# A layer's list scheduler gets longer step durations, and a stretch for VectorE beside GpSimd

## The chip, the core and the metric

The kernel runs on one core of a Trainium2 chip. The metric is the device time of one execution in microseconds (us). In the profile the engines are called PE (TensorE matmul), PEld (its weight loads), DVE (VectorE), ACT (ScalarE), POOL (GpSimd) and SP (SyncE, which issues most DMAs).

## What is computed

One decoder layer over 1024 tokens of width 1024, batch 1, float32:

```python
mod = silu(c) @ w_ada + b_ada            # -> sh1, sc1, gt1, sh2, sc2, gt2
h = rms_norm(x, g_pre_mix) * (1 + sc1) + sh1
proj = h @ w_in                          # -> u | bg | cg | v, 512 columns each
y_a = s5_mixer(u, ...)                   # 32 complex state spaces, GELU, sigmoid GLU
y_b = bg * causal_dwconv(cg * v, conv_w) # width 3
y = concat(head_rms_norm(y_a), head_rms_norm(y_b))
x = x + gt1 * rms_norm(y @ w_out, g_post_mix)
h = rms_norm(x, g_pre_ffn) * (1 + sc2) + sh2
a, v = split(causal_dwconv(h @ w_up, ffn_conv_w))
x = x + gt2 * rms_norm((silu(a) * v) @ w_down, g_post_ffn)
```

## The kernel before, in words

Everything lies with channels on the 128 partitions and tokens along the free axis, so x is 8 tiles (`x`, k = 0 to 7) of 128 x 1024. Every large product is made in three passes (`mm3`, the matmuls of L475, L477 and L479): both factors are split into a high and a low part, and high x high, high x low and low x high are added up in PSUM. PSUM has three buffers of 128 x 1024 (`big`) and two of 128 x 512 (`sm`). A weight tile is loaded by SP (`w`), cast to its high part by ACT (L461) and its low part taken by DVE or POOL (L381); it lies in one of three buffers `hl`.

The work up to about 560 us of the span runs in these stages, which overlap:

- **u product** (`t_u`): u = x @ w_in's first 512 columns, made from x scaled by its columns alone (`X`), with the token's norm applied afterwards (`t_u_out`). What the shift sh1 adds to it, the bias, is made per pair of tiles from the shift's high and low parts `shl` (L692 to L695, one column each) in `t_bias` (L801, L802): bias 0 to 3, each adding to `bs`, and at the end `bu` (L816, L818). A bias group frees the weight buffer that it shared with the u product. The last 512 tokens of the last 128 columns come behind, as `uh2`.
- **h** (`t_h`, L714 to L725): the normalised x with scale and shift, split in two parts.
- **projection** (`t_proj`): twelve products of h, the matmuls `big<-h,hl`, 48 each. The first two run in turns on two PSUM buffers. `t_conv` makes of each three of them a tile of group b: `p`, the taps on DVE, and at its end `yb` (L867), which frees the PSUM buffer.
- **tables of the state space**, made by POOL for four sets of eight groups: rotations `Pt`, `CL`, `WB`, and for the tap kernels `Bd` (L1072 to L1077), which PE multiplies (L1084, L1086, called taps here).
- **per set** (`t_set`): `V` (L1201, from u and the turned `WB`, L1126), four products on DVE that free its PSUM buffer (L867 `sv<-big,Pt`), a scan, `Y` (L1253, L1258), and GELU in two DVE steps (`z<-z,big`) and two of ACT.
- **GLU and norms**: `t_glu`, `t_gate`, the heads' statistics (L1378), and their expansion (L1421).
- **ada dots** (L631 on DVE, L633 on POOL): the columns of mod, one per 128 x 1024 tile of weights.
- **output product** (`big<-yh,hl`), then the channel sub-layer, whose products fill PE from about 560 us to the end.

The order is not written out by hand. Each piece of work above is a thread, a Python generator that yields a step (engine, planned duration) before it emits the step's instructions. `Flow` is a list scheduler: it keeps a planned time at which each engine is free, takes the engine and time at which the next step could start, and among the threads that could start within 0.02 us the one with the best number in `PRIO`. Waits for other threads, for buffers and for landed loads are planned too. Some steps may go to DVE or POOL (`SITES`), and go where they are planned to end first. The order in which `Flow` comes to the steps is the order of the instructions on each engine, and a step planned too late or too early stays there: each engine executes its queue in order. The durations come from `D_`, `A_` and `G_` (DVE, ACT and POOL, by the elements n per partition) and `M_` (PE).

Of the kernel before, what the change touches and what calls it, by code (L numbers as in the profile page):

```python
# [24 lines left out]
H = 512  # L25
# [176 lines left out]
class Flow:  # L202
# [85 lines left out]
    def run(self, until=None):  # L288

        while True:  # L290
            self._settle()
            if until is not None and until.t is not None:
                return
            ready = [th for th in self.threads if th[4][0] in ("run", "load", "pick")]
            if not ready:
                break
            plan = [(self._choice(th), th) for th in ready]
            t0, e = min((c[0], c[1]) for c, _ in plan)
            (start, e, cost), th = min(
                ((c, th) for c, th in plan if c[1] == e and c[0] <= t0 + 0.02), key=lambda p: p[1][:2]  # L300
            )
            end = self._pe_end(start, cost) if e == "pe" else start + cost
            self.free[e] = end
            if th[4][0] == "load":
                th[3] = start
                th[5] = end + LAND
            else:
                th[3] = end
            th[6] = e
            self._step(th, e if th[4][0] == "pick" else None)  # L310
        assert not self.threads, [(t[0], t[1], t[4], t[2].__name__, t[3]) for t in self.threads]
# [3 lines left out]
def hybrid_layer(ctx, tc, xT, w_adaT, w_ada0, w_u, w_bcv, w_out, w_up, w_down, glu_w, vec, ssm, con, out):  # L315
    nc = tc.nc
    outB = out.rearrange("(b p d) -> b p d", p=P, d=D)
    pe, dve, act, pool = nc.tensor, nc.vector, nc.scalar, nc.gpsimd
# [22 lines left out]
    def big(shape=(P, 1024)):  # L341
        return pbig.tile(list(shape), F32, tag="big", name=nm("big"))

    def small():
        return psm.tile([P, H], F32, tag="sm", name=nm("sm"))
# [7 lines left out]
    def k2(s="t"):  # L353
        return kp2.tile([P, H], F32, tag="k2", name=nm(s))
# [6 lines left out]


    def D_(n):
        return ("run", "dve", 0.07 + 1.04e-3 * n)

    def A_(n):
        return ("run", "act", 0.094 + 0.833e-3 * n)

    def G_(n):
        return ("run", "pool", 0.15 + 2.1e-3 * n)  # L370

    def M_(n):
        return ("run", "pe", n)
# [97 lines left out]
    def mm3(outs, wh, wl, xh, xl, start, stop):  # L471

        n = len(outs)
        for i in range(n):
            pe.matmul(outs[i], wh, xh[i], start=start, stop=False)  # L475
        for i in range(n):
            pe.matmul(outs[i], wh, xl[i], start=False, stop=False)  # L477
        for i in range(n):
            pe.matmul(outs[i], wl, xh[i], start=False, stop=stop)  # L479
# [257 lines left out]
    def t_u():  # L737
        yield ("wait", ev_X[0])
        yield ("get", "big", 3)
        yield ("get", "sm")  # L740
        up = [big() for _ in range(3)]
        uh = small()
        uo = [[t[:, :H], t[:, H:]] for t in up] + [[uh]]
        yield ("get", "k2")
        bs = k2("bs")[:2]
        for k in range(KD):
            yield ("wait", ev_X[k])
            w = wev["u", k // 2]
            yield ("wait", w[0])
            hl = w[1]  # L750
            for c4 in range(NT):
                n = len(uo[c4])
                o = (k % 2) * H + c4 * P
                if c4 == 0:
                    yield M_(0.215 * n)
                    for i in range(n):
                        pe.matmul(uo[0][i], hl[:, 0, o : o + P], X[k][0][i], start=k == 0, stop=False)
                    yield ("wait", ev_Xl[k])
                    yield M_(0.43 * n)
                    for i in range(n):  # L760
                        pe.matmul(uo[0][i], hl[:, 0, o : o + P], X[k][1][i], start=False, stop=False)
                    for i in range(n):
                        pe.matmul(uo[0][i], hl[:, 1, o : o + P], X[k][0][i], start=False, stop=k == KD - 1)
                else:
                    yield M_(0.6465 * n)
                    mm3(uo[c4], hl[:, 0, o : o + P], hl[:, 1, o : o + P], X[k][0][:n], X[k][1][:n], k == 0, k == KD - 1)
            fl.put("k2", 2)
            if k % 2:
                fl.spawn(t_bias(k // 2, hl, bs), PRIO["t_bias"])
        fl.fire(ev_u2)  # L770
        for c4 in (3, 0, 1, 2):
            fl.spawn(t_u_out(c4, uo[c4] + [None]), PRIO["t_u_out"])
        w = wev["u3",]
        yield ("wait", w[0])
        hl = w[1]
        yield ("get", "sm")
        uh2 = small()
        for k in range(KD):
            ks = slice(k * P, (k + 1) * P)
            yield M_(0.6465)  # L780
            mm3([uh2], hl[:, 0, ks], hl[:, 1, ks], X[k][0][1:], X[k][1][1:], k == 0, k == KD - 1)
            fl.put("k2", 2)
        fl.put("hl")
        fl.fire(ev_ups)
        ev_ups.tile = uh2
# [527 lines left out]
    def t_proj():  # L1313
        yield ("wait", ev_ups)

        for group in [bc_order[:PROJ_GROUP]] + [[t] for t in bc_order[PROJ_GROUP:]]:
            tiles_ = []
            for k in range(KD):
                ks = slice(k * P, (k + 1) * P)
                yield ("wait", ev_h[k])  # L1320
                for i, (n, c4) in enumerate(group):
                    if k == 0:
                        w = wev["p", n + c4]
                        yield ("wait", w[0])
                        yield ("get", "big")
                        tiles_.append((big(), w[1]))
                    o, hl = tiles_[i]
                    yield M_(1.293)
                    mm3([o[:, :H], o[:, H:]], hl[:, 0, ks], hl[:, 1, ks], hT[k][0], hT[k][1], k == 0, k == KD - 1)
            for (n, c4), (o, _) in zip(group, tiles_):  # L1330
                fl.put("hl")
                proj_ev[n + c4].tile = o
                fl.fire(proj_ev[n + c4])
        fl.put("k2", 4 * KD)
# [107 lines left out]
    def t_glu():  # L1442
        for s in range(NT):
            yield ("wait", sets[s]["z"])
        yield ("get", "sm")
        ev_stat["a"].tile = small()
        for c4 in range(NT):
            w = wev["g", c4 // 2]
            yield ("wait", w[0])
            gl = w[1]  # L1450
            yield ("get", "big")
            o = big()
            oo = [o[:, :H], o[:, H:]]
            for k in range(NT):
                ks = slice((c4 % 2) * H + k * P, (c4 % 2) * H + (k + 1) * P)
                yield M_(1.293)
                mm3(oo, gl[:, 0, ks], gl[:, 1, ks], zs[k][0], zs[k][1], k == 0, k == NT - 1)
            if c4 % 2:
                fl.put("hl")
            fl.spawn(t_gate(c4, o), PRIO["t_gate"])  # L1460
# [77 lines left out]
    def t_out():  # L1538
        for bi, (hf, lo, hi) in enumerate(blocks):
            n = hi - lo  # L1540
            outs, og4 = {}, {}
            so = [[], [Event() for _ in range(NT)]]
            for part, dp in w_seq[bi]:
                w = wev["o", bi - ((part, dp) in (kept(bi - 1) if bi else [])), part, dp]
                yield ("wait", w[0])
                hl = w[1]
                if part == first:
                    yield ("get", "big")
                    outs[dp] = big((P, 2, H))
                for k4_ in range(NT):  # L1550
                    k = k4_ + (0 if part == "A" else NT)
                    yield ("wait", ev_y[k][hf])
                    yield M_(1.293 * n / H)
                    for d2 in range(2):
                        ks = slice(k4_ * 256 + d2 * P, k4_ * 256 + (d2 + 1) * P)
                        mm3(
                            [outs[dp][:, d2, :n]], hl[:, 0, ks], hl[:, 1, ks], [yT[k][0][hf][:, lo:hi]], [yT[k][1][hf][:, lo:hi]],
                            part == first and k4_ == 0, part == last and k4_ == NT - 1,
                        )
                if (part, dp) not in kept(bi):  # L1560
                    fl.put("hl")
                if part == last:
                    og4[dp] = Event()
                    fl.spawn(t_out_evac(bi, n, dp, outs[dp], og4, so, len(og4) - 1), PRIO["t_out_evac"])
            if hi == H:
                fl.put("k2", 4 * KD // 2)
            fl.spawn(t_resid(bi, og4, so), PRIO["t_resid"])
        fl.fire(ev_out)
# [929 lines left out]
```

## Time and profile before

| | us |
|---|---|
| median of 3 runs | 1140.34 |
| lowest and highest | 1136.54, 1142.83 |
| the profiled execution | 1135.78 |
| its span | 1134.0 |
| PE busy | 1049.4 |
| DVE busy | 889.3 |
| ACT busy | 482.9 |
| POOL busy | 473.9 |

The clock granted to TensorE is 0.969 of full speed in the mean. Line 2 of the page cuts the span in 40 slices of 28.35 us; each digit is the busy share of a slice in tenths:

```profile
PE   2988889999897998898999999999999999999996
...
DVE  6769779777998288989888799788888887554763
ACT  4435412322344456565433333333334455454552
POOL 4799445671486134212343444343443220342002
PEclk9979889999898998999999999999999999999999
```

PE is nearly full from the twentieth slice on; ahead of it lie slices at 7 and 8 tenths, with a lower clock in some of them. DVE is at 9 tenths in the fourth slice and in the eleventh and twelfth, POOL in the third and fourth. The chain of waits on the page goes back to 934 us only and tells of the last product alone.

### The profile page before, as it was taken

What the parts mean: (1) busy time and instruction counts of PE and PEld (TensorE: products, weight loads), DVE (VectorE), ACT (ScalarE), POOL (GpSimd) and SP (SyncE); (2) the same over time, 40 slices, a digit from 0 to 9 for tenths busy, and PEclk for the clock granted to TensorE, in tenths of its full rate; (3) what the DMA queues carried; (4) which work ended last, traced back from release to release, by engine and by line L of the source; (5) the groups of instructions that cost most, each with busy time, mean ns of one, the idle gap of its engine ahead of it and who ended that gap; (6) DMA issues with size and microseconds to landing.
All of it is one profiled execution on the core that took longest, in us unless ns stands there. A gap on an engine that the chain in (4) does not pass through costs nothing. (4 is left out here: it accounts for less than half of the span.)

```text
span 1134.0 us, 13972 instructions
## 1 busy us (share of the span) xinstructions
PE 1049.4 (93%) x5012; PEld 848.6 (75%) x5012; DVE 889.3 (78%) x1218; ACT 482.9 (43%) x672; POOL 473.9 (42%) x469
## 2 busy tenths in 40 slices
PE   2988889999897998898999999999999999999996
PEld 2756677778554898687778888888888887888885
DVE  6769779777998288989888799788888887554763
ACT  4435412322344456565433333333334455454552
POOL 4799445671486134212343444343443220342002
PEclk9979889999898998999999999999999999999999
DMA  7633313236754356423552233223323597999337
GB/s 276 233 132 131 113 38 98 79 121 213 254 197 133 126 176 196 158 75 121 186 167 96 72 123 128 79 90 112 112 91 104 207 262 245 261 220 293 117 93 139
DMA packets 88821, 172.07 MB, mean 152 GB/s; under 512 B 8752, under 2 KB 34096, under 8 KB 88752
## 3 DMA queue, kind: packets, MB, share of 16 engines
q1 hardware_dynamic: 80688, 156.50, 41.0%
q0 software_dynamic: 8064, 14.68, 7.8%
q8 instruction: 39, 0.64, 0.2%
q14 instruction: 30, 0.25, 0.1%
HBM read 133.69 MB, written 37.46 MB: 151 GB/s over the span
## 5 line engine op out<-in xcount | busy, mean ns | idle before, releaser
L381 POOL TENSOR_TENSOR hl<-w,hl 128x1024 fp32r<-128x1024 f32 x40 | 102.9, 2575 | 284.7 <-ACT hl L1882 149.0
L381 POOL TENSOR_TENSOR w<-w,w 128x512 f32<-128x512 f32 x57 | 84.2, 1477 | 81.9 <-DVE hl L867 78.9
L1882 ACT CAST hl<-w 128x1024 fp32r<-128x1024 f32 (+1 forms) x65 | 66.5, 1023 | 47.7 <-issue 22.9
L2210 POOL DMA_DIRECT2D wd<-in_w_down_dram x44 | 38.5, 884 | 113.0 <-DMA wd<-in_w_down_dram 45.4
L867 DVE TENSOR_TENSOR wl<-wd,wh 128x512 fp32r<-128x512 f32 x77 | 50.9, 686 | 38.5 <-ACT wh L2214 38.2
L477 PE MATMUL big<-yl,hl 128*128 128x256 f32 (+1 forms) x192 | 63.4, 330 | 7.5 <-POOL yl L381 7.5
L2214 ACT CAST wh<-wd 128x512 fp32r<-128x512 f32 x77 | 46.1, 619 | 53.2 <-DMA wd<-in_w_down_dram 51.3
L870 DVE SCALAR_TENSOR_TENSOR ca<-big,vec,ca 128x896 f32<-128x896 f32 (+1 forms) x92 | 65.2, 740 | 3.2 <-ACT ca L2048 3.1
L475 PE MATMUL big<-h,hl 128*128 128x512 f32 x192 | 63.4, 412 | 3.3 <-ACT h L723 1.5
L867 DVE TENSOR_TENSOR hl<-w,hl 128x1024 fp32r<-128x1024 f32 (+1 forms) x45 | 52.9, 1174 | 16.4 <-ACT hl L1882 16.3
L461 ACT CAST hl<-w 128x1024 fp32r<-128x1024 f32 x43 | 44.9, 1044 | 48.0 <-PE big L479 31.2
L475 PE MATMUL big<-yh,hl 128*128 128x256 f32 (+1 forms) x192 | 64.9, 338 | 0.1
L477 PE MATMUL big<-h,hl 128*128 128x512 f32 x192 | 61.4, 401 | 3.0 <-DVE h L725 3.0
L479 PE MATMUL big<-h,hl 128*128 128x512 f32 x192 | 61.1, 400 | 2.8 <-POOL hl L381 2.8
L479 PE MATMUL big<-yh,hl 128*128 128x256 f32 (+1 forms) x192 | 63.3, 330 | 0.1
L475 PE MATMUL big<-s,hl 128*128 128x512 f32 x160 | 63.2, 395 | 0.0
L477 PE MATMUL big<-s,hl 128*128 128x512 f32 x160 | 63.0, 394 | 0.0
L479 PE MATMUL big<-s,hl 128*128 128x512 f32 x160 | 62.8, 393 | 0.0
L475 PE MATMUL big<-h2h,hl 128*128 128x512 f32 (+1 forms) x160 | 60.2, 376 | 0.0
L870 DVE SCALAR_TENSOR_TENSOR cv<-big,vec,cv 128x896 f32<-128x896 f32 (+1 forms) x84 | 58.5, 740 | 1.3 <-ACT cv L2048 1.3
L477 PE MATMUL big<-h2l,hl 128*128 128x512 f32 (+1 forms) x160 | 59.4, 372 | 0.0
L479 PE MATMUL big<-h2h,hl 128*128 128x512 f32 (+1 forms) x160 | 59.4, 372 | 0.0
(361 smaller groups left out, 3162.2 us busy)
## 6 DMA issues: line engine op xcount, KB each, us to landing
w<-in_w_up_dram SPq DMA_DIRECT2D x44, 512.0 KB, 4.0
w<-g_dr SPq DMA_DIRECT2D x35, 512.0 KB, 6.1
g_dr<-cv SPq DMA_DIRECT2D x53, 256.0 KB, 2.2
wd<-in_w_down_dram SPq DMA_DIRECT2D x44, 256.0 KB, 7.7
wd<-in_w_down_dram POOLq DMA_DIRECT2D x44, 256.0 KB, 6.5
w<-in_w_out_dram SPq DMA_DIRECT2D x20, 512.0 KB, 3.6
WBT<-in_w_adaT_dram SPq DMA_DIRECT2D x16, 512.0 KB, 4.6
w<-in_w_bcv_dram SPq DMA_DIRECT2D x13, 512.0 KB, 3.8
```

Of the source, the lines that this page charges most:

```text
L381: {"dve": dve, "pool": pool}[e].tensor_tensor(o, a, b, op)
L461: act.copy(t[:, 0, :], w)
L475: pe.matmul(outs[i], wh, xh[i], start=start, stop=False)
L477: pe.matmul(outs[i], wh, xl[i], start=False, stop=False)
L479: pe.matmul(outs[i], wl, xh[i], start=False, stop=stop)
L867: (eng or dve).tensor_tensor(o, a, b, op)
L870: dve.scalar_tensor_tensor(o, a, s, b, op0, op1)
L1882: act.copy(t[:, 0, :n], w)
L2210: pool.dma_start(w, block_of(made[1], kk), accum_op=ADD)
L2214: act.copy(hi, w)
```

## The change

The durations that the planner reckons with become longer, and a DVE step that is planned while POOL is planned to be busy counts 1.25 times. The constants of the channel sub-layer's steps stay as they were.

```diff
@@ Flow.run
+            if e == "dve" and self.free.get("pool", 0.0) > start:
+                cost *= 1.25
             end = self._pe_end(start, cost) if e == "pe" else start + cost
@@ D_, A_, G_
-        return ("run", "dve", 0.07 + 1.04e-3 * n)
+        return ("run", "dve", 0.155 + 1.045e-3 * n)
-        return ("run", "act", 0.094 + 0.833e-3 * n)
+        return ("run", "act", 0.19 + 0.84e-3 * n)
-        return ("run", "pool", 0.15 + 2.1e-3 * n)
+        return ("run", "pool", 0.18 + 2.2e-3 * n)
@@ t_u
-                    yield M_(0.6465 * n)
+                    yield M_(0.681 * n)
-            yield M_(0.6465)
+            yield M_(0.681)
@@ t_proj, t_glu
-                    yield M_(1.293)
+                    yield M_(1.362)
@@ the output product
-                    yield M_(1.293 * n / H)
+                    yield M_(1.362 * n / H)
```

PE has 4433 rows in both programs, DVE 1129 before and 1136 now, ACT 637 and 631, POOL 455 and 454. The new program's line numbers are 3 higher behind `Flow.run` (L1084 is L1087, L801 is L804). Its order differs from the old one in many places up to the channel sub-layer; three follow. Names end in the number of their buffer.

PE at the end of the u product, in before (from row 186): the last u matmul, bias 3, uh2, the column sums of the bias, the first h matmul, and 72 h matmuls later the taps.

```order
L479 MATMUL sm_243<-X_381,hl_431 128x512
L801 MATMUL sm_790<-hl_431,shl 2x512
...
L475 MATMUL sm_803<-X_225,hl_683 128x512
...
L816 MATMUL sm_816<-con,bs_244 128x1 x4
...
L475 MATMUL big_879<-h_749,hl_709 128x512
...
L1084 MATMUL sm_1037<-ssm,Bd_1017 32x16 x2
L1086 MATMUL sm_1037<-CL_848,Bd_1017 32x112 x2
```

The same place of PE now (from row 178): the last u matmul, the taps, bias 1, the turned `WB` of set 0, bias 2, uh2, bias 3, the rest of uh2, and the first h matmul.

```order
L482 MATMUL sm_229<-X_404,hl_435 128x512
L1087 MATMUL sm_865<-ssm,Bd_855 32x16 x2
L1089 MATMUL sm_865<-CL_792,Bd_855 32x112 x2
...
L804 MATMUL sm_894<-hl_192,shl 2x512
...
L1129 MATMUL big_891<-con,WB_795 128x128 x8
L804 MATMUL sm_923<-hl_321,shl 2x512
...
L478 MATMUL sm_930<-X_206,hl_904 128x512
...
L804 MATMUL sm_947<-hl_435,shl 2x512
...
L478 MATMUL big_1003<-h_730,hl_931 128x512
```

The taps of set 0 have moved ahead of bias 1 to 3, of all of uh2 and of the first 96 h matmuls; in before bias 1 and 2 (not among the rows) stand within the last u matmuls.

DVE around the last `shl`, in before (from row 102; `nrm` is the norm's Newton steps, `bs` the sum of the biases):

```order
L642 TENSOR_TENSOR mod<-mod,vec 128x1
L403 SCALAR_TENSOR_TENSOR nrm_590<-nrm_590 128x8
L405 SCALAR_TENSOR_TENSOR nrm_590<-nrm_590 128x8
L401 TENSOR_TENSOR nrm_590<-nrm_590 128x8
L695 TENSOR_TENSOR shl<-mod,shl 128x1
```

DVE around the last `shl` now (rows 110 to 112 and 141 to 144; the 28 rows left out are h and u work too):

```order
L645 TENSOR_TENSOR mod<-mod,vec 128x1
L717 SCALAR_TENSOR_TENSOR x_136<-x_136,col,rb_714 128x512
L717 SCALAR_TENSOR_TENSOR x_164<-x_164,col,rb_714 128x512
...
L717 SCALAR_TENSOR_TENSOR x_320<-x_320,col,rb_714 128x512
L728 SCALAR_TENSOR_TENSOR h_868<-x_299,mod,h_867 128x512
L698 TENSOR_TENSOR shl<-mod,shl 128x1
L728 SCALAR_TENSOR_TENSOR h_871<-x_320,mod,h_870 128x512
```

The last `shl`, for which bias 1 waits, has moved from the norm's steps to the row behind 32 rows of h and u work.

PE at the first sets' V, in before (rows 320 to 328 and 426 to 434, with a statistic, L1378; 96 h matmuls and Y of set 0 lie between the two V):

```order
L1126 MATMUL big_1023<-con,WB_851 128x128 x8
L475 MATMUL big_1121<-h_749,hl_880 128x512
...
L1201 MATMUL big_1123<-UT_882,WBT_1119 64x128 x16
L475 MATMUL big_1121<-h_765,hl_880 128x512
...
L1126 MATMUL big_1194<-con,WB_1124 128x128 x8
L1378 MATMUL sm_1246<-sq_1247,con 64x512 x2
L475 MATMUL big_1390<-h_749,hl_1160 128x512
...
L1201 MATMUL big_1401<-UT_948,WBT_1388 64x128 x16
```

PE there now (rows 320 to 374): V of set 0, 12 h matmuls, V of set 1, 36 h matmuls, V of set 2, and a new product of the projection.

```order
L482 MATMUL big_1014<-h_951,hl_966 128x512
L1129 MATMUL big_1040<-con,WB_934 128x128 x8
L1204 MATMUL big_1143<-UT_1018,WBT_920 64x128 x16
L478 MATMUL big_1146<-h_730,hl_1004 128x512
...
L1204 MATMUL big_1181<-UT_1065,WBT_1168 64x128 x16
L478 MATMUL big_1146<-h_897,hl_1004 128x512
...
L1129 MATMUL big_1244<-con,WB_1182 128x128 x8
L1204 MATMUL big_1290<-UT_1079,WBT_1285 64x128 x16
L478 MATMUL big_1295<-h_730,hl_1133 128x512
```

V of sets 1 and 2 has moved up by 84 and by 144 h matmuls against V of set 0, and Y of set 0 (not among the rows) now comes behind all three.

More of the change, by code (lines that the diff above doesn't have):

```diff
@@ L1455, in t_glu @@
                 ks = slice((c4 % 2) * H + k * P, (c4 % 2) * H + (k + 1) * P)
-                yield M_(1.293)
+                yield M_(1.362)
                 mm3(oo, gl[:, 0, ks], gl[:, 1, ks], zs[k][0], zs[k][1], k == 0, k == NT - 1)
```

## The prediction

> **What bounds the kernel now.** I read the page's list of engines first, then the busy time of each engine in windows cut at the borders of the stages.
>
> ```profile
> PE 1049.4 (93%) x5012; PEld 848.6 (75%) x5012; DVE 889.3 (78%) x1218; ACT 482.9 (43%) x672; POOL 473.9 (42%) x469
> ```
>
> TensorE works for 93% of the span, so the time is the sum of its matmuls and of what it loses. The windows tell where it loses.
>
> ```profile
> core 0: us, PE busy (x) PEld busy (x) DVE busy (x) ACT busy (x) POOL busy (x), PEclk, DMA share, GB/s
> ...
> 86.00:134.00 48.00, 38.78 (x178) 29.00 (x177) 41.06 (x44) 22.61 (x31) 36.66 (x36) 0.89 0.38 122
> 134.00:294.00 160.00, 154.07 (x933) 123.57 (x931) 131.32 (x177) 46.56 (x48) 84.08 (x136) 0.97 0.38 120
> 294.00:350.00 56.00, 42.79 (x152) 26.26 (x152) 54.17 (x61) 21.75 (x26) 41.15 (x18) 0.87 0.63 216
> 350.00:560.00 210.00, 194.27 (x1081) 167.12 (x1080) 169.57 (x245) 109.02 (x177) 61.39 (x31) 0.95 0.44 143
> 560.00:936.00 376.00, 375.31 (x1646) 307.05 (x1645) 318.68 (x376) 153.36 (x176) 148.67 (x96) 1.00 0.39 127
> ```
>
> In each row stand the length, the busy time of PE, PEld, DVE, ACT and POOL, and the clock that TensorE was granted. From 560 to 936 (the channel sub-layer's first products) PE is busy for 375.3 of 376 us at full clock: no order of steps gains there. Before 560 it stands still by turns. From 134 to 350 it is idle for 5.9 + 13.2 = 19.1 us, and the lower clock takes 154.1 x 0.03 + 42.8 x 0.13 = 10.2 us more: **29.3 us** that another order could lose or win. From 350 to 560 it is 15.7 us idle and 194.3 x 0.05 = 9.7 us of clock. The waits of PE from 134 to 350 have these names:
>
> ```profile
> PE big L477 <- POOL yl L381: 7.5, 2, 6.5
> PE sm L1378 <- ACT sq L1373: 5.1, 1, 5.1
> PE sm L1084 <- POOL Bd L1076: 1.7, 2, 1.4
> PE big L1258 <- DVE St L870: 1.5, 1, 1.5
> PE big L1258 <- DVE St L381: 1.5, 1, 1.5
> ```
>
> The first two lie behind DVE (54.2 of 56 us busy from 294 to 350), which works there at the norms of head group b and at ada dots.
>
> **The change, part by part.** No instruction computes anything else: only the planner's numbers differ, so everything is order. Three things of the new order matter.
>
> **1. Taps in front of the projection.** These rows of before, out of the timelines (start, duration, engine, line), give the times of the stage:
>
> ```profile
> 76.14 0.25 DVE L695 TENSOR_TENSOR shl<-mod,shl 128x1 fp32r<-128x1 f32 x1
> ...
> 78.05 0.40 PE L801 MATMUL sm<-hl,shl 128*2 128x512 f32 x1
> ...
> 87.68 0.40 PE L801 MATMUL sm<-hl,shl 128*2 128x512 f32 x1
> ...
> 96.17 0.61 PE L475 MATMUL big<-h,hl 128*128 128x512 f32 x2
> ...
> 122.19 0.70 POOL L1077 TENSOR_SCALAR Bd<-ssm 64x64 f32<-64x64 f32 x1
> ...
> 126.44 0.30 PE L1084 MATMUL sm<-ssm,Bd 128*32 128x16 f32 x4
> ...
> 127.95 0.73 PE L475 MATMUL big<-h,hl 128*128 128x512 f32 x2
> 128.51 0.62 PE L477 MATMUL big<-h,hl 128*128 128x512 f32 x2
> ...
> 133.07 0.61 PE L479 MATMUL big<-h,hl 128*128 128x512 f32 x2
> 133.52 1.03 PE L1126 MATMUL big<-con,WB 128*128 128x128 f32 x8
> ```
>
> In before the u product ends at 87.68, bias and uh2 follow, and h matmuls run from 96.17. The tap kernels of set 0 stand 72 h matmuls later, at 126.44, when Bd (POOL, ready at 122.19 + 0.70 = 122.9) has long been there. In the new order the taps stand directly behind the last u matmul, ahead of bias 1, bias 2, bias 3, uh2 and every h matmul. One 512-wide matmul is 4.56 / 20 = 0.228 (20 lie between 128.51 and 133.07). PE gets there at 87.7 less two bias groups of four matmuls, 8 x 0.228, = 85.9. It executes in order, so **it stands idle until Bd comes at 122.9, some 37 us**. The cause in the order is the one-column step shl of tile 2 (in before the last of all eight is done by 76.4), which now stands on DVE behind 32 rows of h and u work; bias 1 waits for it, and the weight buffers that the biases free gate the rest.
>
> Does Bd come earlier or later? POOL has the split of the fourth u weight more, ahead of its tables, and one projection weight's split less:
>
> ```profile
> 100.66 2.34 POOL L381 TENSOR_TENSOR hl<-w,hl 128x1024 fp32r<-128x1024 f32 x1
> ...
> 124.54 1.21 DVE L381 TENSOR_TENSOR hl<-w,hl 128x1024 fp32r<-128x1024 f32 x1
> ...
> 135.50 1.05 ACT L461 CAST hl<-w 128x1024 fp32r<-128x1024 f32 x1
> ```
>
> Both are of one size, so they cancel; 2.3 either way if one of them falls into a wait. Behind the taps (1.5 us, 126.44 to 127.95) come bias 1 (0.9), then, with the weight buffer it frees, a cast (1.05) and a split (1.21), so uh2 can start at about 127.6; its 24 matmuls and bias 3 take 24 x 0.228 + 0.9 = 6.4, and the first h matmul starts at about **134.0**. By then before had done 96 h matmuls (its PE rows 216 to 319 less the eight of the taps); all else is level, the taps and the first transposes (133.52) included. So PE is behind by 96 x 0.228 = **21.9 us**. The other 15 us of the 37 were lost in before too, in waits and at the low clock from 86 to 134 and in the start of uh2.
>
> **2. V of sets 1 and 2 early.** From 134 on the new order needs the same work, 21.9 us of it more. If it lost nothing at all until 350, it would be level 21.9 - 29.3 = 7.4 us early; so all hangs on its own losses. PE holds three large PSUM buffers. In the new order V1 stands 12 h matmuls behind V0 and V2 another 36 behind that; in before 96 h matmuls and Y0 lay between V0 and V1. The buffers come free by DVE work that has not moved forward with them, as rows of the timelines show
>
> ```profile
> 133.78 1.22 DVE L867 TENSOR_TENSOR p<-p,big 128x1024 f32<-128x1024 f32 x1 [4.89 <-ACT p L1346]
> ...
> 135.88 1.97 PE L1201 MATMUL big<-UT,WBT 128*64 128x128 f32 x32
> ...
> 153.04 1.19 DVE L867 TENSOR_TENSOR yb<-yb,big 128x1024 f32<-128x1024 f32 x1
> 154.23 0.61 PE L1253 MATMUL big<-UT,Tz 128*128 128x128 f32 x4
> ...
> 196.14 0.61 PE L1253 MATMUL big<-UT,Tz 128*128 128x128 f32 x4
> ...
> 201.18 0.73 PE L475 MATMUL big<-h,hl 128*128 128x512 f32 x2
> ```
>
> and of the view by groups (count | busy, mean ns of one | idle before):
>
> ```profile
> L870 DVE SCALAR_TENSOR_TENSOR z<-z,big 128x1024 f32<-128x1024 f32 x8 | 9.7, 1214 | 14.9 <-ACT z L1263 14.9
> L867 DVE TENSOR_TENSOR sv<-big,Pt 128x512 f32<-128x512 f32 x16 | 10.3, 678 | 1.2 <-POOL Pt L381 1.2
> ```
>
> In before DVE took 154.2 - 133.8 = 20.4 us from p to the product yb that frees a buffer; the new order has the same stretch with two 512-wide products more (0.68 each), 21.8. It starts at 134.0 + 21.9 + 0.3 = 156.2, so the buffer is free at 178.0. PE comes to V2 behind transposes (1.0 each, 133.52), V0, V1 (2.0 each) and 48 h matmuls: 155.9 + 2 x 1.0 + 2 x 2.0 + 48 x 0.228 = 172.8, a wait of **5.2**. Then V2 (2.0), 48 h matmuls (10.9) and a statistic of four (0.9) bring Y0 at 191.8, done at 196.8 (Y1 took 201.18 - 196.14 = 5.0). The next h matmuls want V1's buffer, whose four products on DVE stand between the two z steps of Y0's GELU: two ACT passes (1.05 each by the cast above), two z steps (1.2 each) and one product (0.7) after Y0, 5.2, with 0.2 for the hand-overs **5.4**. Y1 then wants V2's buffer, freed by DVE after the next yb (1.2 + 0.7): **1.9**. That makes 12.5 us. In before 19.1 us of idle time came with 10.2 of clock, so with the clock 12.5 x 29.3 / 19.1 = **19.2**. Bounds: 10.6 (only the first two, no clock) and 31.4 (with 5 for two taps and 3 for the z of set 3, which now has 66 h matmuls of cover in place of 108, all with the clock).
>
> **3. Ada dots earlier.** In before 21 of these stand on DVE from 283 to 350; the first and the last are
>
> ```profile
> 283.54 1.23 DVE L631 SCALAR_TENSOR_TENSOR WBT<-WBT,cbc 128x1024 f32<-128x1024 f32 x1 [2.04 <-DMA WBT<-in_w_adaT_dram]
> ...
> 348.28 2.29 DVE L631 SCALAR_TENSOR_TENSOR WB<-WB,cbc 128x1024 f32<-128x1024 f32 x1
> ```
>
> Eight of them come before that now, 8 x 1.2 to 2.3 = 10 to 18 us of DVE time. I take it that the two long waits on sq and yl (5.1 and 7.5) vanish with it; they are part of the 29.3 that I took off. If they stay, 12.6 come back.
>
> The rest of the new order, the eight expansions of head b among the GLU's matmuls and one norm later, has its cover in PE work that waits for nothing. From 350 to 560 I take no difference; 8 us either way, half of the idle time there. From 560 on none. The twelve-odd steps that change between DVE, ACT and POOL (seven rows more on DVE, six fewer on ACT) cost nothing where PE is full, and are within the bounds elsewhere.
>
> **Sum:** 21.9 - 29.3 + 19.2 = **+11.8 us**. Against the profiled execution, 1135.8 (span 1134.0), that is 1147.6; that execution stands 4.6 under the median of the runs shown, 1140.3, so the median after is **1152**.
>
> Why the planner's new factor may not help where it should: the rows of DVE and POOL that met at 100.6.
>
> ```profile
> 100.63 2.92 DVE L725 SCALAR_TENSOR_TENSOR h<-x,mod,h 128x512 fp32r<-128x512 f32 x1
> ...
> 121.93 0.72 DVE L381 TENSOR_TENSOR x<-x,rb 128x512 f32<-128x512 f32 x1
> ```
>
> A 512-wide step with two SBUF inputs takes 0.72 beside small POOL steps, and 2.92 where it met POOL's 2.34 at 100.66: of those 2.20 us more the planner's 1.25 covers 0.18. So DVE's steps are planned too short beside POOL, and what is planned just in time behind them comes late. The Trainium skill ("SBUF — State Buffer", section "Who interferes with whom") says that the pair of ports is locked for the whole instruction and the loser fully blocks; 2.34 + 0.72 = 3.06 is near the 2.92, so the trace agrees. By that rule each meeting costs a POOL instruction: three more meetings with a 128x1024 split in the stretch before yb would make V2's wait 5.2 + 7.0 and the sum, with the clock, about +22.6; by the planner's 1.25 it would stay within 1 us of +11.8.
>
> **Rivals.**
> - **Full price (0.22).** Losses at the upper bound: 21.9 - 29.3 + 31.4 = +24.0, median 1164. The way there: DVE's two-input steps meet POOL's 2.3 us splits three or four times more than in before, as at 100.63, and each delay reaches PE through a buffer. For it: before itself lost 29.3 here. Against: DVE has 28.7 us free from 134 to 294.
> - **Absorbed (0.20).** Losses of 7 rather than 19: the sum is about 0, median 1140. For it: the earlier dots free DVE, and the projection runs with fewer breaks; against it: three buffers and the early V. The same time comes out if the change only reorders what PE would do anyway, with Bd early.
> - **Faster (0.15).** One mechanism: DVE is relieved from 283 to 350 and ahead at 350, so that the waits of 350 to 560 shrink by 8 and 134 to 350 loses only 7: -8, median 1132. It decides once the losses from 134 on fall under 1.7 with 350 to 560 as it was, or under 10 with the 8 us won.
> - **Forecast (0.43).** Slower by 6 to 20, median 1146 to 1160.
>
> Slower by over 0.5% (5.7 us, about what a measurement of this kernel can tell from no change): forecast and full price, 0.65; within 0.5%: 0.20; faster: 0.15. The range leaves out the better half of the faster case and the worst of the full price: 1134 to 1168.
>
> **What would show it.** PE idle from about 86 to 123 with Bd as the releaser, and the first h matmul near 134 (before 96): step 1. V2 waiting for yb and the h matmuls behind Y0 for sv, 5 to 6 us each: step 2. No 5 us wait on sq and no 6.5 on yl, and dots on DVE before 283: step 3. The last statistic of head a starts 12 us later than in this row of before:
>
> ```profile
> 349.76 1.98 PE L1378 MATMUL sm<-Tz,con 128*64 128x512 f32 x4
> ```
>
> The prediction is wrong if Bd is there well before 115, if PE's loss from 134 to 350 stays under 10, or if 350 to 560 differs by more than 8.

## The result and the profile after

The changed kernel takes 1194.70 us (median of 4 runs, 1191.97 to 1195.49) against 1139.59 (4 runs, 1136.54 to 1142.83): the ratio is **1.0482**, with a 95% interval of 1.0453 to 1.0511. That is 55 us slower. The forecast was 1152 in a range of 1134 to 1168: the direction came out, the size did not. The profiled execution took 1195.49, its span is 1193.7, and the mean granted clock is 0.947.

The list of engines and the slices of the page, for the changed kernel (the span in 40 slices of 29.84 us):

```profile
PE 1051.2 (88%) x5012; PEld 847.6 (71%) x5012; DVE 862.0 (72%) x1219; ACT 480.5 (40%) x670; POOL 469.5 (39%) x469
...
PE   4760998999889998896999999999999996999996
...
PEclk9985998999989998898999999999999997999998
```

PE works as long as before (1051.2 and 1049.4 us) in a span that is 59.7 longer, so the loss is idle time. (The profiled execution of before is the fastest of its four and that of the changed kernel the slowest of its four, so the profiles differ by 59.7 us and the medians by 55.) The fourth slice holds no PE work, and the 19th (537 to 567 us) and the 34th (985 to 1015 us) stand at 6, where before had 8 and 9. DVE's busy time has fallen by 27 us with one instruction more, and the kernel is slower all the same.

The windows of before's table once more, now of the changed kernel, and one for the down product:

```profile
86.00:134.00 48.00, 12.59 (x81) 8.37 (x82) 36.29 (x44) 19.00 (x27) 40.14 (x43) 0.61 0.10 26
134.00:294.00 160.00, 148.59 (x883) 118.52 (x882) 109.58 (x160) 41.41 (x44) 79.01 (x133) 0.97 0.39 128
294.00:350.00 56.00, 44.95 (x198) 32.87 (x197) 45.62 (x68) 16.76 (x17) 13.94 (x9) 0.88 0.77 251
350.00:560.00 210.00, 190.05 (x1039) 157.41 (x1037) 161.87 (x223) 107.49 (x173) 73.81 (x37) 0.96 0.38 122
560.00:936.00 376.00, 366.75 (x1594) 298.04 (x1595) 292.91 (x359) 139.86 (x159) 151.48 (x92) 0.98 0.34 112
936.00:1190.00 254.00, 234.01 (x1003) 190.14 (x1001) 154.10 (x240) 118.94 (x193) 50.00 (x57) 0.96 0.76 199
```

PE is busy for 12.6 us from 86 to 134 (before 38.8), and from 560 to 936, where it had been full, it now loses 9 us. Since windows cut at fixed times mix stages, this table has the starts of the matmuls that border them, from the timelines of PE:

| matmul | before | after | later by |
|---|---|---|---|
| first of h | 96.2 | 134.8 | 38.6 |
| last statistic of head a | 349.8 | 376.2 | 26.4 |
| last of the output product | 459.2 | 480.1 | 20.9 |
| first of the down product | 910.3 | 958.5 | 48.2 |
| last of the down product | 1125.3 | 1184.0 | 58.7 |

So 20.9 us are lost up to the end of the output product, 27.3 in the product with `w_up` (called the up stage here), 10.5 in the down product, and 1 behind it. The waits of PE in the changed kernel have these names (total, times, longest):

```profile
PE sm L1087 <- POOL Bd L1079: 39.9, 2, 38.8
...
PE big L2260 <- ACT hl L1885: 11.4, 1, 11.4
...
PE sm L1381 <- ACT sq L1376: 7.0, 1, 7.0
PE sm L2126 <- ACT sn L2021: 6.0, 1, 6.0
PE sm L482 <- DVE hm L870: 5.2, 3, 1.9
...
PE sm L1424 <- DVE hl L873: 4.1, 1, 4.1
PE big L480 <- DVE h2l L873: 4.0, 3, 1.8
```

The hole at Bd is there, and of the waits that the prediction wrote off the one on yl is gone but for 0.8 us, while that on sq has grown from 5.1 to 7.0. New, or grown from under 2 us, are `sn`, `hm` and `h2l` in the up stage, and `hl` in the down product.

### The profile page after: what moved, and what is told of

Read it like the earlier page. It is cut to its first block, busy times and chain, and to the rows that moved or that the text cites. A ratio compares the mean times of both kernels' runs of the same rounds, so it can differ in the third digit from the quotient of the medians.

```text
span 1193.7 us, 13944 instructions
## 1 busy us (share of the span) xinstructions
PE 1051.2 (88%) x5012; PEld 847.6 (71%) x5012; DVE 862.0 (72%) x1219; ACT 480.5 (40%) x670; POOL 469.5 (39%) x469
## 4 chain that ended last, share of the span: by engine, by line
PE 45%; DVE 6%; DMA 2%; issue 1%; ACT 1%; SPq 0%; DVEq 0%; ACTq 0%
PE big L478 5%; PE big L480 5%; PE big L482 5%; PE sm L482 5%; PE sm L478 4%; PE sm L480 4%; PE big L2260 4%; PE big L2262 4%; PE big L2261 4%; DMA wd<-in_w_down_dram 2%; PE sm L2260 1%; PE sm L2262 1%; PE sm L2261 1%; DVE ca L873 1%; DVE s L873 1%
## 5 line engine op out<-in xcount | busy, mean ns | idle before, releaser
L384 POOL TENSOR_TENSOR hl<-w,hl 128x1024 fp32r<-128x1024 f32 x39 | 99.6, 2554 | 309.6 <-ACT hl L464 159.1
L1885 ACT CAST hl<-w 128x1024 fp32r<-128x1024 f32 (+1 forms) x65 | 66.5, 1023 | 97.2 <-PE big L482 24.2
L2213 POOL DMA_DIRECT2D wd<-in_w_down_dram x44 | 38.5, 879 | 122.0 <-DVE wl L870 63.7
L478 PE MATMUL big<-h,hl 128*128 128x512 f32 x192 | 61.7, 403 | 5.3 <-DVE z L873 4.9
L478 PE MATMUL big<-yh,hl 128*128 128x256 f32 (+1 forms) x192 | 63.3, 330 | 0.0
L482 PE MATMUL big<-yh,hl 128*128 128x256 f32 (+1 forms) x192 | 61.8, 322 | 0.0
L2260 PE MATMUL big<-wh,hl 128*128 128x512 f32 x130 | 51.2, 394 | 11.4 <-ACT hl L1885 11.4
L480 PE MATMUL big<-h,hl 128*128 128x512 f32 x192 | 60.1, 395 | 0.0
```

The lines of the kernel that those rows point to most:

```text
L384: {"dve": dve, "pool": pool}[e].tensor_tensor(o, a, b, op)
L1885: act.copy(t[:, 0, :n], w)
L2260: pe.matmul(o, gh, wh, start=kk == 0, stop=False)
```

## The experiments

Sixteen kernels ran. This table gives each one's time against the kernel before in the same session, then, from its profile, the start of the output product's last matmul, the time from there to ACT's first copy `sn<-sm` in the up stage, the length of the up stage and of the down product (between first and last matmul), and PE's one long wait for `hl` in it.

| run | median us | ratio | output's end | to first sn | up | down | hl |
|---|---|---|---|---|---|---|---|
| before | 1139.6 | 1 | 459.2 | 64.9 | 451.1 | 215.0 | 1.6 |
| after | 1194.7 | 1.0482 | 480.1 | 80.3 | 478.4 | 225.5 | 11.4 |
| x1 | 1181.5 | 1.0353 | 469.8 | 83.7 | 475.2 | 225.7 | 12.4 |
| x2 | 1188.7 | 1.0413 | 482.3 | 80.3 | 467.9 | 228.4 | 13.6 |
| x3 | 1152.9 | 1.0108 | 462.0 | 66.7 | 452.8 | 226.9 | 12.4 |
| x4 | 1154.9 | 1.0123 | 474.1 | 62.9 | 446.4 | 224.9 | 11.7 |
| x5 | 1190.0 | 1.0434 | 480.5 | 79.9 | 477.9 | 221.4 | 6.7 |
| x6 | 1151.5 | 1.0096 | 476.4 | 66.7 | 448.0 | 214.7 | 1.8 |
| x7 | 1166.8 | 1.0237 | 458.4 | 82.3 | 469.3 | 226.0 | 11.6 |
| x8 | 1146.6 | 1.0065 | 460.6 | 65.1 | 450.7 | 223.5 | 7.6 |
| x9 | 1173.3 | 1.0331 | 480.8 | 80.0 | 467.2 | 215.3 | 1.3 |
| x10 | 1161.7 | 1.0216 | 454.1 | 66.5 | 463.8 | 226.8 | 13.0 |
| x11 | 1140.0 | 1.0018 | 458.1 | 66.7 | 451.6 | 219.4 | 4.1 |
| x12 | 1163.1 | 1.0237 | 469.5 | 83.1 | 468.2 | 216.1 | 1.9 |
| x13 | 1160.5 | 1.0210 | 487.1 | 65.5 | 448.0 | 214.4 | 1.5 |
| x14 | 1162.4 | 1.0219 | 452.8 | 82.2 | 472.6 | 224.7 | 10.6 |
| x15 | 1143.5 | 1.0055 | 460.1 | 69.3 | 455.2 | 219.6 | 3.7 |
| x16 | 1147.6 | 1.0091 | 453.1 | 66.7 | 453.8 | 227.3 | 12.7 |

The 95% intervals reach 0.0016 to 0.0037 to either side. The columns behind the ratio come from one execution each; that of x10 took 1155.8 us, 5.9 less than its median. Below, "the planner's last stage" begins when the forms `s` of the up stage's input have been planned (line `fl.run()` at the end), and "from the output product" begins earlier, at the last statistic of head a, two calls of `stage` ahead.

**First four: the hole, the factor, and the DVE durations.** In the changed kernel, x1 lets the one-column `shl` go first, x2 takes the factor away in the last stage, and x4 puts the old `D_` back. x3 is the kernel before with the factor in the last stage alone.

```diff
x1 -    "t_sh": 9,
x1 +    "t_sh": 3.4,
x2 -                cost *= 1.25
x2 +                cost *= self.stretch
x2 +    fl.stretch = 1.0
x2      fl.run()
x4 -        return ("run", "dve", 0.155 + 1.045e-3 * n)
x4 +        return ("run", "dve", 0.07 + 1.04e-3 * n)
```

> The changed kernel with one number different: the priority of the thread that makes shl (t_sh) is 3.4 in place of 9, ahead of the h work. In the order shl then comes before the h work, bias 1 and 2 before the end of the u product, and the taps behind all of uh2 but the last three h-free rows. Theory A (several causes: the late shl costs the 22 us of the hole, and the 1.25 factor costs some 24 us by itself in the channel sub-layer): PE no longer waits 39 us for Bd, the time is about 1165 to 1178. Rival B (one cause: all that is lost later follows from the hole): about 1140 to 1150.

> The changed kernel with the factor of 1.25 on DVE switched off from the last stage of the planner on (the channel sub-layer, from about PE row 1955); all before stays. Theory A: the waits on hm and wf and the 11.4 us wait on hl at 997 us go, the time falls by some 20 to 24 us to about 1171 to 1175. Rival B: the losses there come from the lateness, the time stays within 5 us of 1195.

> The kernel before with nothing but the factor of 1.25 on DVE, switched on in the last stage of the planner (the channel sub-layer). All rows ahead of PE row 1963 are those of before. Theory A: the losses of the channel sub-layer come without any hole, about 20 to 24 us, time about 1160 to 1164. Rival B: within 5 us of 1140.

> The changed kernel with the old durations of DVE steps (0.07 + 1.04e-3 n); the factor and the new ACT, POOL and PE durations stay. shl is early (DVE rows up to 105) and the taps stand 54 h matmuls behind uh2. Theory A: no hole, losses of the channel sub-layer remain: about 1160 to 1170. Rival B: about 1140.

None of the four came out as its Theory A said: x1 stands 3 us above that range, x4 5 us below it, and x2 and x3 lie between the two alternatives. x1 wins 13 us, not the whole loss of the stage: the first h matmul starts at 121.6 rather than 134.8, since other waits take the hole's place. Of its waits of PE:

```profile
PE sm L819 <- DVE bs L870: 14.7, 1, 14.7
...
PE sm L1087 <- POOL Bd L1079: 7.7, 2, 4.4
```

x2 wins 6 us: the waits for `hm` and `wf` are gone and the up stage is 10.5 shorter, but the down product still waits for `hl`, and is 2.9 longer. x3 shows that the factor alone makes that wait grow, from 1.6 to 12.4 us, in a kernel which has none of the other losses. x4 wins 40 us; with old DVE durations the up stage has no loss at all, and the wait for `hl` stays.

**The wait for `hl` in the down product.** On ACT, the casts of the down product's weights (`wh<-wd`) stand in one queue with the last evictions of the up stage (L2048 in before, L2051 now). ACT's timeline in before:

```profile
914.73 1.11 ACT L2048 ACTIVATE cv<-big,vec 128x1024 f32<-128x1024 f32 x1
...
923.75 1.12 ACT L2048 ACTIVATE ca<-big,vec 128x1024 f32<-128x1024 f32 x1
```

ACT's in the changed kernel:

```profile
978.66 2.19 ACT L2217 CAST wh<-wd 128x512 fp32r<-128x512 f32 x4 [2.73 <-DMA wd<-in_w_down_dram]
980.75 1.11 ACT L2051 ACTIVATE cv<-big,vec 128x1024 f32<-128x1024 f32 x1
...
982.79 1.11 ACT L2051 ACTIVATE ca<-big,vec 128x1024 f32<-128x1024 f32 x1
```

And the queue of SP there (its durations are those of the issue):

```profile
976.39 16.92 SPq L363 DMA_DIRECT2D g_dr<-cv  x5
...
993.91 1.46 SPq L363 DMA_DIRECT2D w<-g_dr  x3
```

In before 18 such casts stand ahead of the last eviction, now 27 (28 or 29 in x2, x4, x10, x14 and x16). Each may wait for its load, and so the two evictions come 22.2 and 24.2 us behind the first down matmul (958.55) rather than 4.4 and 13.4 behind it (910.3). The last gated products go out through memory (`g_dr<-cv`) and back (`w<-g_dr`) before PE can use them: PE stands until 997.5. x5 (the changed kernel) and x8 (x3) hold the casts back by a gate: no nineteenth cast until the last eviction is planned.

```diff
+                    if n == 18:
+                        yield ("wait", ev_last)
```

> The changed kernel, with the down projection's weight thread held back: from its 19th block on it waits until the planner has come to the last eviction of the up products, so that 18 casts of down weights stand on ACT ahead of that eviction (as in the kernel before) in place of 27. All before the down projection stays. Theory C (the 11.4 us wait on hl at 997 us comes from those nine casts, each of which waits for its load): the wait falls under 3 us and the time by 8 to 12, to about 1184. Rival D (the loads saturate the DMA engines there, and the order on ACT is no matter): the wait stays, time within 3 us of 1195.

> The kernel x3_factor_late_only (the kernel before with the factor in the channel sub-layer) with the weight thread held back as in x5_gate: 18 casts ahead of the last eviction in place of 27. Theory C: the 12.4 us wait on hl goes, the time falls from 1153 to about 1141 to 1144. Rival D: it stays at 1153.

The wait falls from 11.4 to 6.7 and from 12.4 to 7.6 us, where both expectations wanted it gone or under 3, so the casts are about 40% of it. What remains shows on ACT, here from the waits of ACT in x8:

```profile
ACT cv L2052 <- DMA g_dr<-cv: 8.0, 1, 8.0
```

The eviction needs a buffer `cv`, which comes free when the sums of an earlier pair are made on DVE and stored; and these stand on DVE behind 18 low parts of down weights, the last ten of them right ahead of the sums (DVE's timeline in x8):

```profile
922.89 6.10 DVE L871 TENSOR_TENSOR wl<-wd,wh 128x512 fp32r<-128x512 f32 x10
928.91 0.68 DVE L871 TENSOR_TENSOR cv<-cv 128x512 f32<-128x512 f32 x1
```

x11 is x8 with the sums of the last pairs ahead of them:

```diff
-                fl.spawn(t_sums(i // 2, even, r["b"]), PRIO["t_sums"])
+                fl.spawn(t_sums(i // 2, even, r["b"]), 2 if i > NFF - 4 else PRIO["t_sums"])
```

> The kernel x8_late_factor_gate with the sums of the last two pairs (cv<-cv, cv<-cv,gs on DVE) at priority 2 in place of 14, so that they stand ahead of the weight splits on DVE, as in the kernel before, and free the buffer cv for which ACT's last eviction waited 8 us. Theory C2 (of the 12 us in the down projection half is the nine casts and half these sums): the wait on hl falls from 7.6 to under 3 us and the time from 1146.6 to about 1140 to 1143. Rival D (what is left is the load of the DMA engines): it stays at 1146.

The wait is down to 4.1 (before 1.6), the down product to 219.4 (x3: 226.9), and the time, 1139.97, stands within 0.2% of the kernel before. So in the kernel of x3 both queues, ACT's casts and DVE's sums, make most of this loss: 7.5 of 11.9 us in the down product. In the changed kernel only the gate on the casts ran (x5), and it took 4.1 of 10.5. x11 is no gain on the kernel before, and no other version here is one.

**Which durations.** x6 gives the kernel before the new PE durations alone, x7 the new `D_` and `A_` alone; a line of each stands for its kind.

```diff
x6 -                    yield M_(0.6465 * n)
x6 +                    yield M_(0.681 * n)
x7 -        return ("run", "act", 0.094 + 0.833e-3 * n)
x7 +        return ("run", "act", 0.19 + 0.84e-3 * n)
```

> The kernel before with the longer PE durations alone (0.681, 1.362); no factor, DVE, ACT and POOL as before. Its order has the last shl at DVE row 151 and the taps at PE row 184, 41 rows ahead of the first h matmul, as in the changed kernel, and 18 weight casts ahead of the last eviction. Theory C: the hole costs by itself what it costs in the changed kernel up to the end of the output product, 21 to 27 us, and the down projection nothing: about 1160 to 1168. Rival E (it is the DVE durations that make the order bad): within 6 us of 1140.

> The kernel before with the longer DVE and ACT durations, no factor, POOL and PE as before. Its order has shl early (DVE row 106) and the taps at PE row 264, behind uh2 and 48 h matmuls, but 27 weight casts ahead of the last eviction. Theory C: no hole, the down projection loses 10 to 12: about 1150 to 1158. Rival E: the DVE durations make it bad as in the changed kernel, 1170 and more.

PE durations that are 5% longer open a hole by themselves, in another place (a row of x6's waits of PE):

```profile
PE big L1126 <- DVE WB L381: 27.2, 2, 22.8
```

x6 has its first h matmul at 130.2 and the output's end 17.2 us late; in the up stage and the down product it loses nothing. It is 11.6 us slower in all. x7 is the opposite: no loss up to the output's end, 18 in the up stage and 11 in the down product. The two together are 11.6 + 26.9 = 38.5 of the 55. Neither was expected so: x6 lies below its 1160 to 1168, since its hole costs 17.2 us and not 21 to 27 and part of that is won back behind it, and x7, whose up stage was not expected to lose, lies above its 1150 to 1158.

**Lateness or order.** The up stage of the changed kernel starts 21 us late, and it could lose time because of that or because of its own order. x9 is the changed kernel with old numbers (`D_`, `A_`, `G_`, no factor) in the last stage, x10 the kernel before with the new ones there; x12 is x9 with x1's edit; x13 and x14 are as x9 and x10, with the switch at the output product; x15 switches `D_` alone there, x16 `A_`, `G_` and the factor. `A_`, `G_` and the factor get the same switch as `D_` in these lines.

```diff
x9  -        return ("run", "dve", 0.155 + 1.045e-3 * n)
x9  +        return ("run", "dve", (0.07 + 1.04e-3 * n) if fl.late else (0.155 + 1.045e-3 * n))
x9  +    fl.late = True
x9       fl.run()
x13 +    fl.run(until=ev_stat["a"])
x13 +    fl.late = True
x13      stage(ev_sp, mix, "a", {"s4": 2 * NT, "ca": NCA, "wf0": 1, "hm0": 1}, side="right")
```

> The changed kernel with the old DVE, ACT and POOL durations and no factor from the planner's last stage on (the channel sub-layer, which uses these three functions too); all PE rows up to about 1950, with the hole, stay. Theory F (the numbers that hold in the last stage cost the channel sub-layer's 27 us and the down projection's 10): both go but for some 4, the time is about 1157 to 1165. Rival B (they follow from PE's being late against the plan): the time stays above 1185.

> The kernel before with the new DVE, ACT and POOL durations and the factor in the planner's last stage alone; no hole. Theory F: the whole loss of the channel sub-layer and of the down projection without the hole, 1140 + 30 to 37 = 1170 to 1177. Rival B: under 1153.

> x9_late_old with shl at priority 3.4 as in x1_sh_early: new numbers up to the channel sub-layer, without the hole in front of the taps. Theory: the first h matmul comes near 122 as in x1_sh_early, 13 us less than x9_late_old: about 1145 to 1152. If the new numbers up to there are better than the old ones but for the hole, it is under 1140.

> The changed kernel with the old DVE, ACT and POOL durations and no factor from the last statistic of head a on (PE row 1037); up to there, with the hole, its order is the changed kernel's. Theory G (what is lost behind the output product comes from the numbers that hold from there on): from the last output matmul to the first down matmul 451 us as before (479 in the changed kernel), and 215 in the down projection; the time is about 1155 to 1163, against 1173 for x9_late_old, where the switch came later. Rival B (it follows from the order handed over with the hole): 1170 and more.

> The kernel before with the new DVE, ACT and POOL durations and the factor from the last statistic of head a on; up to there its order is that of before, so no hole. Theory G: the channel sub-layer loses 24 to 27 and the down projection 10 to 12: about 1172 to 1180. Rival B: within 5 us of x10_late_new or faster, 1150 to 1160.

> As x14_new_from_output with the new DVE durations alone (no factor, ACT and POOL old). 18 weight casts ahead of the last eviction. If it is the DVE durations (x4_old_dve lost nothing in the channel sub-layer, x7_dve_act 18): 16 to 18 us there, nothing in the down projection, about 1154 to 1160. If DVE's durations matter only with ACT's: within 5 us of 1140.

> As x14_new_from_output with the new ACT and POOL durations and the factor, DVE durations old. 28 weight casts ahead of the last eviction. If it is the DVE durations: nothing lost in the channel sub-layer, 10 to 12 in the down projection, about 1150 to 1153. Otherwise 1165 and more.

x13 starts its up stage 28 us later than before and needs 448.0 and 214.4 us for the rest, as before does. x14 starts 6.4 us early and loses 21.5 and 9.7. So **lateness by itself costs nothing there, with the old numbers in force; the new numbers do, without any lateness**. Whether lateness adds something to the new numbers no run tells. x13 came where it was expected; x14 lost less than expected (1162.4, not 1172 to 1180), and x9 and x10 lie between their alternatives. x9 against x13 tells when: with the switch only in the last stage, the down product is healed (215.3) and 16 us of the up stage's loss stay. What is planned between the two switches is the output product, the normalised input of the up stage (`h2h`, `h2l`) and the forms `s`. The forms show a difference. ACT's timeline there in before:

```profile
522.21 1.93 ACT L1833 CAST s<-og 128x256 fp32r<-128x256 f32 x6
524.05 0.58 ACT L2018 COPY sn<-sm 128x512 f32<-128x512 f32 x1
```

in the changed kernel:

```profile
554.91 2.86 ACT L1836 CAST s<-og 128x256 fp32r<-128x256 f32 x9 [5.63 <-DVE og L870]
...
560.46 0.58 ACT L2021 COPY sn<-sm 128x512 f32<-128x512 f32 x1
```

and in x13:

```profile
552.58 0.58 ACT L2022 COPY sn<-sm 128x512 f32<-128x512 f32 x1
```

The copy `sn` frees one of the two small PSUM buffers. It stands on ACT behind the casts of the forms, which wait for `og` from DVE: 80.3 us behind the end of the output product, against 64.9 in before and 65.5 in x13. In every run in which it comes 79.9 us or more behind, the up stage needs 467 us or more; in every other at most 464. That the late forms are the cause is argued from this: no run moves them alone. PE's waits for `sn` in the up stage are 8.4 us in x9 and 1.9 in x13, and those for `h2l` 3.6 and none. x15 and x16 do not show the late forms: `D_` alone gives 69.3 and 4 us of loss in the up stage, the rest alone 66.7 and 2.6, and only `D_` and `A_` together (x7) put the forms late. Their gains and losses, 6.3 and 10.4 us in all, add up to 17, and together (x14) they cost 25. x15 came where it was expected if DVE's durations matter only with ACT's; x16 came under its range. In x15 the down product is 4.5 us longer although 18 casts stand ahead of the last eviction, as in before; why stays open.

x10 shows the other part of the up stage: with the forms in time, new numbers in the last stage cost 12.7 us in the execution profiled, and x2 has taken 10.5 of such a loss away by the factor alone. x3, where the factor stands in the last stage with old durations, loses only 1.7. So it takes the factor and the longer durations.

x12 beats x9 by 10 us, as x1 beat the changed kernel by 13; at 1163.1 it is far from the expected 1145 to 1152. No run takes the factor out of the whole program, so what it costs up to the output product stays open.

## Why the prediction was too small

**What bounds the kernel: right.** All but 1.8 of the 59.7 us are idle time of PE. But "375.3 of 376 us at full clock: no order of steps gains there" was read as if no order could lose there either. A stage that is full in one order tells what that order hides, not that any order would.

**Step 1, the hole: right within 2 us.** Bd came at 121.1 (expected 122.9), the wait was 38.8 (some 37), the first h matmul started at 134.8 (134.0). Of PE's timeline in the changed kernel:

```profile
121.11 0.29 PE L1087 MATMUL sm<-ssm,Bd 128*32 128x16 f32 x2 [38.83 <-POOL Bd L1079]
...
134.79 0.39 PE L478 MATMUL big<-h,hl 128*128 128x512 f32 x1
...
175.84 0.40 PE L1204 MATMUL big<-UT,WBT 128*64 128x128 f32 x3 [2.23 <-issue]
...
191.63 0.60 PE L1256 MATMUL big<-UT,Tz 128*128 128x128 f32 x3
...
201.73 1.19 PE L478 MATMUL big<-h,hl 128*128 128x512 f32 x2 [4.88 <-DVE z L873]
...
233.02 0.35 PE L1256 MATMUL big<-UT,Tz 128*128 128x128 f32 x1 [1.41 <-DVE yb L870]
...
329.63 1.12 PE L1381 MATMUL sm<-sq,con 128*64 128x512 f32 x2 [6.96 <-ACT sq L1376]
```

**Step 2, the early V: nearly right.** Y0 came at 191.6 (191.8), the h matmul behind it waited 4.9 (5.4), Y1 1.4 (1.9). V2 waited 2.2, not 5.2, and the trace names no releaser.

**Step 3, the ada dots: half wrong.** Of the two waits that were to vanish, the one on yl did (0.8 of 7.5 left) and the one on sq did not. "Eight of them come before that now" counted rows of the order, not time. The hole moved all of DVE's rows too, so in time hardly anything moved. The windows of DVE for the dots' line alone (each dot is two rows), in the changed kernel:

```profile
134.00:283.00 149.00, 14.61 (x20) 0.97 0.40 129
283.00:362.00 79.00, 32.16 (x44) 0.91 0.64 208
```

and in before:

```profile
134.00:283.00 149.00, 13.17 (x18) 0.97 0.35 109
283.00:362.00 79.00, 38.44 (x44) 0.89 0.56 193
```

Ten dots instead of nine come before 283, and 22 still come behind it. So the wait on sq stayed. DVE's timeline ahead of it shows why:

```profile
318.91 1.23 DVE L634 SCALAR_TENSOR_TENSOR WBT<-WBT,cbc 128x1024 f32<-128x1024 f32 x1 [2.02 <-DMA WBT<-in_w_adaT_dram]
...
320.19 1.22 DVE L634 SCALAR_TENSOR_TENSOR Pt<-Pt,cbc 128x1024 f32<-128x1024 f32 x1
...
321.34 4.81 DVE L873 SCALAR_TENSOR_TENSOR yb<-p,vec,yb 128x896 f32<-128x896 f32 x4
...
326.07 1.21 DVE L634 SCALAR_TENSOR_TENSOR WB<-WB,cbc 128x1024 f32<-128x1024 f32 x1
...
327.22 1.21 DVE L870 TENSOR_TENSOR yb<-yb,big 128x1024 f32<-128x1024 f32 x1
```

The taps of the tile for which PE waits stand behind two dots, the first of which waits 2.0 us for its load, and a third dot stands between them and `yb`. Reckoned as the prediction did, the losses from 134 to 350 (with a wait of 4.1 for the `hl` of L1424 among them) are 11.4 + 11.1 = 22.5 us of idle time and 148.6 x 0.03 + 45.0 x 0.12 = 9.9 of clock: 32.4, where the sum had 19.2. The statistic came 26.4 us later rather than 12; 13.2 more on the sum gives 25.0. The 32.4 lie 1 us beyond the upper bound of 31.4, for another reason than the bound had. 5.5 us were won back by the end of the output product, so the stretch that the sum is about lost 20.9 us instead of 11.8. The term for the clock in this reckoning, busy time times the missing share of the clock, is not a measured loss: up to the end of the output product PE was busy for 382.8 us in the changed kernel and for 394.0 in before.

**"From 350 to 560 I take no difference ... From 560 on none": the step that failed.** Behind the end of the output product the kernel lost 38.8 us more, two thirds of the whole. It rested on a sentence ahead of the prediction, that the constants of the channel sub-layer stay as they were. That holds only of its products on PE and of the DVE steps that use `E_`, which had the longer duration before. Its evictions and casts on ACT use `A_`, its taps and the steps that make `h2l` use `D_`, its splits on POOL use `G_`, and the factor is in `Flow.run` for every step. The runs put in its place: 16 us in the up stage from what is planned between the output product and the last stage (x9 against x13), where the late forms are the likeliest cause, though no run moves them alone; some 11 there by the factor with the longer durations in the last stage (x2, x10); and 10.5 in the down product, of which the casts ahead of the last evictions made 4.1 (x5) and DVE's sums, by x8 and x11, probably most of the rest. With the 20.9 of before that these are 58, beside a difference of 58.7 at the last down matmul.

**The rivals.** Absorbed and faster fell. "Full price" had the direction, but neither its place nor its mechanism: it wanted three or four more meetings of DVE and POOL in the projection, and DVE was busy for 155 us from 134 to 350, not 185, with nearly as many rows. Lateness carried on into the up stage, the obvious reading of the new waits, fell with x13 as a cause by itself. Nor need the new numbers be worse as durations. For 1024 elements `D_` gives 1.225 us (before 1.135), where DVE's splits took 1.221 in the mean; `A_` gives 1.05 (0.95), where ACT's casts took 1.049; `G_` gives 2.43 (2.30), where POOL's splits took 2.55; and 1.362 for six matmuls is 0.227 each (0.216), where the prediction read 0.228. All are nearer to the trace than the old ones, and the order made with them is worse: even the PE durations alone, 5% longer, cost 11.6 us.

What stays open is why `D_` and `A_` put the forms late only together, and the last 7 us or so by which the changed kernel exceeds x13's and x14's losses taken together (23 + 25 of 55). The stages tell where these lie: x13 and x14 together make the output product's end 21.5 us later (20.9 in the changed kernel) and the down product 9.0 longer (10.5), but the up stage only 18.4 longer, where the changed kernel needs 27.3 more.

## What to carry to other kernels

A change of a planner's numbers is a change to every step that is planned with them: list the call sites of each constant down to the last stage before a stage is called untouched, and look in the new order at the queues of the engines that evict there, even where PE has no idle time in the old trace. Count moved work in time, not in rows, once an early hole shifts all engines. And to tell whether a late stage suffers from an early loss or from its own order, switch the numbers at the border between them, both ways: two runs told here what each does alone, and left open what they do together.

## What was not expected of the hardware

DVE and POOL met outside of the stretch that the prediction looked at, too. POOL's timeline of the changed kernel, and then DVE's:

```profile
549.06 2.41 POOL L384 TENSOR_TENSOR hl<-w,hl 128x1024 fp32r<-128x1024 f32 x1 [15.56 <-ACT hl L1885]
551.54 1.35 POOL L384 TENSOR_TENSOR w<-w,w 128x512 f32<-128x512 f32 x1
```

```profile
547.12 0.87 DVE L873 SCALAR_TENSOR_TENSOR s<-og,tsh,s 128x256 fp32r<-128x256 f32 x2
...
549.12 4.07 DVE L873 SCALAR_TENSOR_TENSOR s<-og,tsh,s 128x256 fp32r<-128x256 f32 x2
```

Two 256-wide steps took 0.87 us together before POOL's split began and 4.07 beside POOL: 3.2 more, near the 2.41 + 1.35 of POOL's two. That agrees with the rule of the Trainium skill ("SBUF — State Buffer", section "Who interferes with whom") that the prediction drew on, by which the loser is fully blocked. It lies in the late forms of the changed kernel; what such a meeting costs PE no run here has measured by itself.

The clock granted to TensorE fell with PE's idle time: 0.61 in the window that held the hole (before 0.89), and 0.96 in the last (936 to 1190), which holds the wait for `hl`; before's from 936 to 1130 had 1.00. How dear this is differs by stage. From 480 to 958, the up stage, PE was busy for 454.3 us at 0.97, against 442.9 at 0.99 for before's stage from 459 to 910, so 11.3 of the 27.3 us are longer busy time and the rest is waiting. In the down product the clock fell from 1.00 to 0.97 too, which would be 6.4 us of 213.5, yet the busy time of the same 925 matmuls rose only from 212.2 to 213.5. The mean over a window counts idle stretches as well (0.50 from 89.5 to 119.4 us, where PE does nothing), so a low mean is not by itself lost time, and over the whole span the busy time rose by only 1.8 us.
